# Group softmax on one core: tiles computed in place, twelve buffers, loads and stores on two queues

## The chip, the cores and the metric

The kernel runs on one NeuronCore of a Trainium2 chip; the other cores are idle. The metric is device time in microseconds, the median of three runs. The engines that matter here are VectorE (DVE in the profile), ScalarE (ACT), SyncE (SP, which only issues transfers) and the 16 DMA engines that move data between HBM and the on-chip memory, SBUF. An engine runs its instructions in order, and an instruction that waits holds up all that stand behind it on its engine.

## The reference

```python
def reference(x):                       # x: (4, 4096, 4352) float32
    B, N, D = x.shape
    G = 8
    Dg = D // G                         # 544
    x_g = x.reshape(B, N, G, Dg)
    x_g = x_g - x_g.max(axis=-1, keepdims=True)
    exp = np.exp(x_g)
    out = exp / exp.sum(axis=-1, keepdims=True)
    return out.reshape(B, N, D).astype(np.float32)
```

Each row of 4352 numbers falls into 8 groups of 544, and each group gets its own softmax. The input is 285 MB and the output is as large.

## The kernel before

The 16384 rows are cut into 128 tiles of 128 rows, one row to a partition; a tile is 128 x 4352 float32, 17408 bytes to a partition and 2176 KB in all. One loop runs over the tiles. For each tile SP loads `xt` (line 32); VectorE takes the 8 negated group maxima in one instruction, `mx` (line 35); ScalarE runs 8 activations (line 40), each of which writes the exponentials of one group into a second tile `ot` and their sum into a column of `sm`; VectorE takes the reciprocals `rs` (line 49) and multiplies each group of `ot` by its own (line 51); SP stores `ot` (line 52).

The pool has 4 buffers for each name, so 4 of `xt` and 4 of `ot`. A load of tile t+4 waits for ScalarE to have read tile t's `xt`, and an activation of tile t+4 overwrites an `ot` whose store must have landed. All loads and all stores are issued by SP, in one line of instructions. The framework orders the instructions of each engine itself, so the order on an engine is not that of the loop. It also tells DMAs apart by eight completion semaphores, DMAHW0 to DMAHW7, given out in turn; a DMA that is given a semaphore waits until the one that had it before has landed.

Of the kernel before, what the change touches and what calls it, by code (L numbers as in the profile page):

```python
# [1 line left out]

# [4 lines left out]


@with_exitstack
def kernel(  # L10
    ctx: ExitStack,
    tc: tile.TileContext,
    x: bass.AP,
    out: bass.AP,
):
    nc = tc.nc
    G = 8
    P = 128
    xf = x.flatten_outer_dims()
    of = out.flatten_outer_dims()  # L20
    N, D = xf.shape
    Dg = D // G
    xg = xf.rearrange("n (g d) -> n g d", g=G)
    og = of.rearrange("n (g d) -> n g d", g=G)
    ntiles = N // P

    pool = ctx.enter_context(tc.tile_pool(name="io", bufs=4))
    small = ctx.enter_context(tc.tile_pool(name="small", bufs=4))

    for t in range(ntiles):  # L30
        xt = pool.tile([P, G, Dg], mybir.dt.float32)
        nc.sync.dma_start(out=xt, in_=xg[t * P:(t + 1) * P])  # L32

        mx = small.tile([P, G], mybir.dt.float32)
        nc.vector.reduce_max(out=mx, in_=xt, axis=mybir.AxisListType.X, negate=True)  # L35

        sm = small.tile([P, G], mybir.dt.float32)
        ot = pool.tile([P, G, Dg], mybir.dt.float32)
        for g in range(G):
            nc.scalar.activation(  # L40
                out=ot[:, g, :],
                in_=xt[:, g, :],
                func=mybir.ActivationFunctionType.Exp,
                bias=mx[:, g:g + 1],
                scale=1.0,
                accum_out=sm[:, g:g + 1],
            )
        rs = small.tile([P, G], mybir.dt.float32)
        nc.vector.reciprocal(out=rs, in_=sm)  # L49
        for g in range(G):  # L50
            nc.vector.tensor_scalar_mul(out=ot[:, g, :], in0=ot[:, g, :], scalar1=rs[:, g:g + 1])  # L51
        nc.sync.dma_start(out=og[t * P:(t + 1) * P], in_=ot)  # L52


# [1 line left out]
_INS = ['x']  # L56
_OUTS = [((4, 4096, 4352), 'float32')]


# [23 lines left out]
```

## Time and profile before

| | us |
|---|---|
| median of 3 runs | 1601.17 (1600.88 to 1601.21) |
| the profiled execution: span from first to last instruction | 1599.5 |
| VectorE busy | 1048.2 (66%) |
| ScalarE busy | 760.8 (48%) |
| DMA engines, share of the span (queue q1) | 85.6% |
| DMA rate over the span | 357 GB/s |

The profiled execution's own time is not given beside its span; the span is 1.67 us under the median of the runs, and that difference is taken as what lies around it. Busy time is the time in which an engine works. The idle time in front of an instruction is put down to what ended it, the releaser. For a DMA, the profile gives the time from its issue to its landing, when the data is there and its semaphore has counted up. A transfer's rows are spread over all 16 DMA engines.

### The profile page before, as it was taken

What the parts mean: (1) busy time and instruction counts of PE and PEld (TensorE: products, weight loads), DVE (VectorE), ACT (ScalarE), POOL (GpSimd) and SP (SyncE); (2) the same over time, 40 slices, a digit from 0 to 9 for tenths busy, and PEclk for the clock granted to TensorE, in tenths of its full rate; (3) what the DMA queues carried; (4) which work ended last, traced back from release to release, by engine and by line L of the source; (5) the groups of instructions that cost most, each with busy time, mean ns of one, the idle gap of its engine ahead of it and who ended that gap; (6) DMA issues with size and microseconds to landing.
All of it is one profiled execution on the core that took longest, in us unless ns stands there. A gap on an engine that the chain in (4) does not pass through costs nothing.

```text
span 1599.5 us, 4255 instructions
## 1 busy us (share of the span) xinstructions
DVE 1048.2 (66%) x1280; ACT 760.8 (48%) x2049; POOL 0.2 (0%) x4
## 2 busy tenths in 40 slices
DVE  7568655587556775567765677656776567765566
ACT  6245444455444554445544355443554435544354
POOL 0000000000000000000000000000000000000000
DMA  8888998888988889888898888998889988898887
GB/s 362 355 341 349 376 383 346 337 349 369 390 348 341 349 355 390 361 337 353 351 383 369 341 349 355 374 378 336 344 359 376 376 342 341 362 375 371 344 340 312
DMA packets 36897, 570.71 MB, mean 357 GB/s; under 512 B 4096, under 2 KB 4096, under 8 KB 4096
## 3 DMA queue, kind: packets, MB, share of 16 engines
q1 hardware_dynamic: 36864, 570.44, 85.6%
q14 instruction: 33, 0.27, 0.0%
HBM read 285.21 MB, written 285.21 MB: 357 GB/s over the span
## 4 chain that ended last, share of the span: by engine, by line
DMA 33%; DVE 27%; ACT 26%; issue 10%; SPq 1%; DVEq 0%; ACTq 0%
DMA xt<-in_x_dram 33%; ACT ot L40 26%; DVE ot L51 18%; DVE mx L35 8%; DVE rs L49 1%; SPq L32 1%; SPq L52 1%; DVEq L78 0%; ACTq L78 0%
## 5 line engine op out<-in xcount | busy, mean ns | idle before, releaser
L40 ACT ACTIVATE ot<-xt,mx 128x544 f32<-128x544 f32 x1024 | 750.7, 734 | 817.8 <-DVE mx L35 667.3
L35 DVE TENSOR_REDUCE mx<-xt 128x8 f32<-128x4352 f32 x128 | 599.5, 4683 | 426.0 <-DMA xt<-in_x_dram 426.0
L51 DVE TENSOR_SCALAR ot<-ot,rs 128x544 f32<-128x544 f32 x1024 | 434.3, 499 | 4.5
L40 ACT ACTIVATION_READ_ACCUMULATOR ot<-xt,mx 128x1 f32 x1024 | 191.4, 187 | 0.0
L49 DVE RECIPROCAL rs<-sm 128x8 f32<-128x8 f32 x128 | 25.5, 199 | 113.3 <-ACT ot L40 113.3
L40 ACT ACT_TABLE_LOAD x1 | 1.3, 1283 | 9.7 <-DMA xt<-in_x_dram 9.7
L67 POOL MEMSET const-uint8-127<- 128x1 uint8 x1 | 0.1, 102 | 0.0
L67 POOL MEMSET const-bfloat16-1.0<- 128x1 bf16 x1 | 0.1, 101 | 0.0
L67 POOL MEMSET const-float32-0.0<- 128x1 f32 x1 | 0.1, 98 | 0.2 <-issue 0.2
L67 POOL MEMSET const-float32-1.0<- 128x1 f32 x1 | 0.1, 98 | 0.0
## 6 DMA issues: line engine op xcount, KB each, us to landing
xt<-in_x_dram SPq DMA_DIRECT2D x128, 2176.0 KB, 17.1
out_dram<-ot SPq DMA_DIRECT2D x128, 2176.0 KB, 6.6
```

Of the source, the lines that this page charges most:

```text
L32: nc.sync.dma_start(out=xt, in_=xg[t * P:(t + 1) * P])
L35: nc.vector.reduce_max(out=mx, in_=xt, axis=mybir.AxisListType.X, negate=True)
L40: nc.scalar.activation(out=ot[:, g, :], in_=xt[:, g, :], func=mybir.ActivationFunctionType.Exp, bias=mx[:, g:g + 1], scale=1.0, accum_out= ...
L49: nc.vector.reciprocal(out=rs, in_=sm)
L51: nc.vector.tensor_scalar_mul(out=ot[:, g, :], in0=ot[:, g, :], scalar1=rs[:, g:g + 1])
L52: nc.sync.dma_start(out=og[t * P:(t + 1) * P], in_=ot)
L67: nc = _bacc.Bacc("TRN2", target_bir_lowering=False, num_devices=1)
```

## The change

The exponentials are written over the tile that was loaded, and the scaled values over these, so the second tile is gone and the one pool has 12 buffers of the loaded tile. The order of the instructions is written out by hand: twelve loads first, then in each round the maximum and the exponentials of tile i, and the scaling and the store of tile i-1. Loads are issued by SP, stores by ScalarE. A load of tile i+12 takes the buffer of tile i and so waits for tile i's store to have landed. The arithmetic and the shapes of all instructions are as before.

```diff
+    NBUF = 12
-    pool = ctx.enter_context(tc.tile_pool(name="io", bufs=4))
+    pool = ctx.enter_context(tc.tile_pool(name="io", bufs=NBUF))
-    for t in range(ntiles):
-        xt = pool.tile([P, G, Dg], mybir.dt.float32)
-        nc.sync.dma_start(out=xt, in_=xg[t * P:(t + 1) * P])
+    def load(i):
+        xt = pool.tile([P, G, Dg], f32, name="xt")
+        tiles[i] = xt
+        nc.sync.dma_start(out=xt, in_=xg[i * P:(i + 1) * P])
-        mx = small.tile([P, G], mybir.dt.float32)
+    def store(i, eng):
+        eng.dma_start(out=og[i * P:(i + 1) * P], in_=tiles.pop(i))
+
+    def expo(i):
+        xt = tiles[i]
+        mx = small.tile([P, G], f32, name="mx")
         nc.vector.reduce_max(out=mx, in_=xt, axis=mybir.AxisListType.X, negate=True)
-        ot = pool.tile([P, G, Dg], mybir.dt.float32)
...
             nc.scalar.activation(
-                out=ot[:, g, :],
+                out=xt[:, g, :],
                 in_=xt[:, g, :],
...
+    def scale(i):
+        xt = tiles[i]
+        rs = small.tile([P, G], f32, name="rs")
+        nc.vector.reciprocal(out=rs, in_=sums.pop(i))
         for g in range(G):
-            nc.vector.tensor_scalar_mul(out=ot[:, g, :], in0=ot[:, g, :], scalar1=rs[:, g:g + 1])
-        nc.sync.dma_start(out=og[t * P:(t + 1) * P], in_=ot)
+            nc.vector.tensor_scalar_mul(out=xt[:, g, :], in0=xt[:, g, :], scalar1=rs[:, g:g + 1])
+
+    with tc.manual_schedule():
+        for i in range(NBUF):
+            load(i)
+        for i in range(nt + 1):
+            if i < nt:
+                expo(i)
+            if i:
+                scale(i - 1)
+                store(i - 1, nc.scalar)
+                if i - 1 + NBUF < nt:
+                    load(i - 1 + NBUF)
```

What SP issues in the middle of the kernel before, with the semaphores that each DMA waits for (DMAHW are those of DMAs, DVE and Activation those of the engines; the number in a name tells buffers apart):

```order
L32 DMA xt_686<-in_x_dram 128x4352 [waits DMAHW2_49,Activation_49]
L32 DMA xt_711<-in_x_dram 128x4352 [waits DMAHW3_49,Activation_49]
L32 DMA xt_736<-in_x_dram 128x4352 [waits DMAHW4_49,Activation_49]
L32 DMA xt_761<-in_x_dram 128x4352 [waits DMAHW5_49,Activation_49]
L52 DMA out_0_dram<-ot_691 128x4352 [waits DMAHW6_49,DVE_49]
L52 DMA out_0_dram<-ot_716 128x4352 [waits DMAHW7_49,DVE_49]
L52 DMA out_0_dram<-ot_741 128x4352 [waits DMAHW0_49,DVE_49]
L52 DMA out_0_dram<-ot_766 128x4352 [waits DMAHW1_49,DVE_49]
```

Four loads stand together, and behind them four stores that wait for VectorE. The same engine in the middle of the changed kernel:

```order
L37 DMA xt_1008<-in_x_dram 128x4352 [waits DMAHW7_49,DMAHW6_49,DVE_49]
L37 DMA xt_1032<-in_x_dram 128x4352 [waits DMAHW1_49,DMAHW0_49,DVE_49]
L37 DMA xt_1056<-in_x_dram 128x4352 [waits DMAHW3_49,DMAHW2_49,DVE_49]
L37 DMA xt_1080<-in_x_dram 128x4352 [waits DMAHW5_49,DMAHW4_49,DVE_49]
L37 DMA xt_1104<-in_x_dram 128x4352 [waits DMAHW7_49,DMAHW6_49,DVE_49]
```

SP now holds loads alone. Each waits for the load that had its semaphore four loads earlier (the odd numbers) and for the store that empties its buffer (the even ones). ScalarE's line in the changed kernel, some rounds later, with the store of each tile between the activations:

```order
L40 DMA out_0_dram<-xt_984 128x4352 [waits DMAHW4_49,DVE_49]
L49 ACTIVATE xt_1032,sm_1276<-xt_1032,mx_1274 128x544 [waits DMAHW1_49,DVE_49,Activation_49]
L49 ACTIVATE xt_1032,sm_1276<-xt_1032,mx_1274 128x544 x7
L40 DMA out_0_dram<-xt_1008 128x4352 [waits DMAHW6_49,DVE_49]
L49 ACTIVATE xt_1056,sm_1300<-xt_1056,mx_1298 128x544 [waits DMAHW3_49,DVE_49,Activation_49]
L49 ACTIVATE xt_1056,sm_1300<-xt_1056,mx_1298 128x544 x7
L40 DMA out_0_dram<-xt_1032 128x4352 [waits DMAHW0_49,DVE_49]
```

In the kernel before ScalarE issued no DMA. Now a store stands behind the exponentials of the next tile, waits for the scaling of its own tile and for the store four earlier, which had its semaphore, and holds up the exponentials behind it.

## Rows read from the trace of the kernel before

**Rows 1.** The page's head and part 1: busy us, share, instructions.

```profile
span 1599.5 us, 4255 instructions
DVE 1048.2 (66%) x1280; ACT 760.8 (48%) x2049; POOL 0.2 (0%) x4
```

**Rows 2.** The page's parts 3 and 6: DMA queues; a load's KB, us to landing.

```profile
q1 hardware_dynamic: 36864, 570.44, 85.6%
q14 instruction: 33, 0.27, 0.0%
...
xt<-in_x_dram SPq DMA_DIRECT2D x128, 2176.0 KB, 17.1
```

**Rows 3.** Waits, whole span: us in total, times, longest; SP's own last.

```profile
ACT ot L40 <- DVE mx L35: 667.3, 33, 21.6
DVE mx L35 <- DMA xt<-in_x_dram: 426.0, 64, 13.2
...
SPq L52 <- DVE ot L51: 1397.0, 127, 24.1
```

**Rows 4.** Timeline of SP from 500 to 560 us: start, us, what it issued.

```profile
499.97 6.50 SPq L52 DMA_DIRECT2D out_dram<-ot  x2
506.56 4.01 SPq L32 DMA_DIRECT2D xt<-in_x_dram  x4
533.38 22.77 SPq L52 DMA_DIRECT2D out_dram<-ot  x4
556.25 3.95 SPq L32 DMA_DIRECT2D xt<-in_x_dram  x4
```

**Rows 5.** Timeline of VectorE, same stretch, idle time before each in brackets.

```profile
518.97 4.69 DVE L35 TENSOR_REDUCE mx<-xt 128x8 f32<-128x4352 f32 x1 [12.85 <-DMA xt<-in_x_dram]
524.16 4.69 DVE L35 TENSOR_REDUCE mx<-xt 128x8 f32<-128x4352 f32 x1 [0.51 <-DMA xt<-in_x_dram]
...
529.97 3.39 DVE L51 TENSOR_SCALAR ot<-ot,rs 128x544 f32<-128x544 f32 x8
...
538.10 3.39 DVE L51 TENSOR_SCALAR ot<-ot,rs 128x544 f32<-128x544 f32 x8
...
546.23 3.39 DVE L51 TENSOR_SCALAR ot<-ot,rs 128x544 f32<-128x544 f32 x8
```

**Rows 6.** Windows of that stretch; the last two columns: DMA share, GB/s.

```profile
510.00:512.00 2.00, 0.00 (x0) 0.00 (x0) 0.00 (x0) 1.00 1.20 383
512.00:514.00 2.00, 0.00 (x0) 0.00 (x0) 0.00 (x0) 1.00 0.85 287
514.00:528.00 14.00, 8.52 (x2) 4.26 (x11) 0.00 (x0) 1.00 0.99 424
540.00:542.00 2.00, 2.00 (x5) 2.00 (x7) 0.00 (x0) 1.00 0.00 0
...
542.00:547.00 5.00, 4.96 (x4) 2.83 (x9) 0.00 (x0) 1.00 0.99 418
```

**Rows 7.** Line 52, issue to landing: the stores issued at 506.1 and 1585.9.

```profile
DMA to landing us min/median/max: 7.6/7.6/7.6
...
DMA to landing us min/median/max: 6.6/6.6/6.6
```

**Rows 8.** Chain of waits, the 16 ScalarE instructions of one tile: start, us.

```profile
546.17 5.97 ACT ot L40 x16
```

**Rows 9.** Timeline of the first 30 us.

```profile
0.73 2.80 SPq L32 DMA_DIRECT2D xt<-in_x_dram  x4
...
9.69 4.68 DVE L35 TENSOR_REDUCE mx<-xt 128x8 f32<-128x4352 f32 x1 [9.69 <-DMA xt<-in_x_dram]
...
26.04 0.19 ACT L40 ACTIVATION_READ_ACCUMULATOR ot<-xt,mx 128x1 f32 x1
```

**Rows 10.** Timeline of SP in the last 40 us.

```profile
1577.77 14.64 SPq L52 DMA_DIRECT2D out_dram<-ot  x3
```

**Rows 11.** Line 52 over the whole span: ns min/median/max of an issue.

```profile
L52 SPq DMA_DIRECT2D out_dram<-ot x128: 332/343/348, 24.1 to 1592.1; - x128
```

More of the change, by code (lines that the diff above doesn't have):

```diff
@@ L24 @@
     og = of.rearrange("n (g d) -> n g d", g=G)
-    ntiles = N // P
-    pool = ctx.enter_context(tc.tile_pool(name="io", bufs=4))
+    nt = N // P
+    pool = ctx.enter_context(tc.tile_pool(name="io", bufs=NBUF))
     small = ctx.enter_context(tc.tile_pool(name="small", bufs=4))
-    for t in range(ntiles):
-        xt = pool.tile([P, G, Dg], mybir.dt.float32)
-        nc.sync.dma_start(out=xt, in_=xg[t * P:(t + 1) * P])
-        mx = small.tile([P, G], mybir.dt.float32)
+    f32 = mybir.dt.float32
+    tiles = {}
+    sums = {}
+    def load(i):
[7 more added lines that the diff above has]
+        mx = small.tile([P, G], f32, name="mx")
         nc.vector.reduce_max(out=mx, in_=xt, axis=mybir.AxisListType.X, negate=True)
-        sm = small.tile([P, G], mybir.dt.float32)
-        ot = pool.tile([P, G, Dg], mybir.dt.float32)
+        sm = small.tile([P, G], f32, name="sm")
+        sums[i] = sm
         for g in range(G):
             nc.scalar.activation(
-                out=ot[:, g, :],
+                out=xt[:, g, :],
                 in_=xt[:, g, :],
@@ L47 @@
             )
-        rs = small.tile([P, G], mybir.dt.float32)
-        nc.vector.reciprocal(out=rs, in_=sm)
+    def scale(i):
+        xt = tiles[i]
+        rs = small.tile([P, G], f32, name="rs")
+        nc.vector.reciprocal(out=rs, in_=sums.pop(i))
         for g in range(G):
-            nc.vector.tensor_scalar_mul(out=ot[:, g, :], in0=ot[:, g, :], scalar1=rs[:, g:g + 1])
-        nc.sync.dma_start(out=og[t * P:(t + 1) * P], in_=ot)
+            nc.vector.tensor_scalar_mul(out=xt[:, g, :], in0=xt[:, g, :], scalar1=rs[:, g:g + 1])
[10 more added lines that the diff above has]
+                    load(i - 1 + NBUF)
 _INS = ['x']
```

## The prediction

> **What bounds the kernel now.** I read the engines' busy time first [rows 1]. VectorE works 1048 us and ScalarE 761 us of 1599.5, so neither is full. The DMA queue is at 85.6% [rows 2], which is high, and the question is whether the rest is overhead inside the transfers or time in which nothing is in flight. The windows answer it [rows 6]: between 514 and 528 us, when only loads are in flight, the 16 engines run at a share of 0.99 and 424 GB/s; between 540 and 542 us they move nothing at all; from 542 to 547 us one store alone runs at 0.99 and 418. The transfers are at a ceiling when there are any, and then there are none.
>
> What a transfer costs at that ceiling is read from VectorE's timeline [rows 5]: it is idle, and starts a maximum at 518.97 and the next at 524.16, each as its load lands. Loads queued back to back land 5.19 us apart. A load is 2176 KB [rows 2], so this is 429 GB/s, one percent above the 424 of the window; the store's 418 is within three percent of it, and I take 5.19 for both.
>
> Why the engines run dry is in SP's timeline [rows 4]. SP issues four loads at 506.56 and the next four at 556.25: a period of 49.69 us for four tiles. In between it issues stores one after another as VectorE finishes tiles, and the waits of SP say how long it stands there: 1397 us in all for line 51 [rows 3]. The next loads are queued behind those stores on SP. VectorE finishes tiles 8.13 us apart (529.97, 538.10, 546.23 in [rows 5]), a store needs only 5.19, and each leaves a gap. Eight transfers of 5.19 are 41.5 us of the 49.69; the other 8.2 us in each of 32 periods, 262 us in all, are what the kernel loses. Then the four loads come together, and VectorE waits 12.85 us for the first of them that it has not yet got. That is most of its 426 us of waiting for loads, and ScalarE's 667 us behind VectorE follows from it [rows 3].
>
> **The change part by part.** Loads no longer stand behind stores. From the written order a load waits for the load four earlier and for the store that empties its buffer, so up to four loads and four stores are in flight. A pair of transfers costs the DMA engines 2 x 5.19 = 10.38 us per tile. Compute needs less: VectorE 8.13 us, ScalarE 5.97 us for its 16 instructions [rows 8] and 0.34 us to issue a store [rows 11], so 6.3 us. The bound moves to the DMA engines as long as a load is always queued.
>
> Is one always queued? The loop that a buffer goes round is, if loads and stores share the engines evenly: four loads at 10.38 us from issue to landing, 41.5; the tile through compute, 14.4 us (load landed at 518.97, its store issued at 533.38 [rows 4, 5]) and 6 us more, since the store now stands behind the next tile's exponentials; four stores, 41.5, and 1.4 for a store's start (it lands 6.6 us after issue when it runs alone [rows 7], of which 5.19 is transfer). That is 105 us. Twelve buffers at 10.38 us give 124.6. So there are buffers to spare, and the spare time is where the added waits sit: a store on ScalarE that waits for an older store holds back the next exponentials, VectorE waits for those, and neither is late for the DMA engines. At the start the first nine loads need only loads to have landed; they keep the engines busy until about 4.5 + 9 x 5.19 = 51 us. The tenth waits for the first store; ScalarE is done with the second tile's exponentials at about 26.2 [rows 9], so that store lands by about 40 even at half rate.
>
> The in-place writes cost nothing that I can see: line 51 already works in place at 3.39 us for eight, and no engine reads the tile that another writes. The hand-written order on VectorE (maximum, then the scaling of the tile before) has the same instructions.
>
> The sum, for the profiled execution:
> - Data starts at 9.69 - 5.19 = 4.5 us [rows 9]: 4.5.
> - 256 transfers at 5.19: 1328.6.
> - The end. When no loads are left, VectorE delivers a tile every 8.13 us and a store takes 5.19, so each store that is not queued by then opens a gap of 2.94. Between none of these (enough stores queued) and twelve (35 us) I take two or three, since four stores are queued then and cover most of the rest: 7.5.
> - Instruction fetches, 0.27 MB [rows 2], now run against a full queue. On one engine alone (429 / 16 = 26.8 GB/s) they would be 10 us, spread over all 0.6; I take 5.
> - From the last store's landing to the end: the last store is issued at 1592.08 (the end of the last three less one issue of 0.33 [rows 10, 11]), lands 6.6 us later, and the span ends at 1599.5: 0.8.
>
> This is 1346.4 us of span, and with the 1.7 us between the span and the median of the runs 1348 us. Against 1599.5 it takes back the 262 us of idle DMA time and gives up some 10 at the end and to instruction fetches.
>
> **The unknown price: loads and stores at the same time.** The trace has almost no stretch of this kind, since one queue carries both in order. It has one junction per period: a store with a load queued right behind it. There the store lands 7.6 us after issue instead of 6.6 [rows 7], and the two windows around it run at 383 and 287 GB/s [rows 6]. So a change from writing HBM to reading it costs up to 1.0 us. In the changed kernel both queues hold work all the time. If the cost vanishes because reads and writes of both kinds overlap evenly, it is 0. If it is paid once for each pair of transfers it is 128 x 1.0 = 128 us, and if it is paid at each of the eight rows that a DMA engine moves of a transfer (36864 packets over 256 transfers and 16 engines are nine each, eight of data and one that signals) it is 1024 us. I take 0, by the row nearest to a full queue, the 424 GB/s at a share of 0.99, and because the junction looks like the emptying of one kind of work before the other has started. This is the weakest step.
>
> No run here shows loads and stores together on two queues; the Trainium skill does ("DMA: Bandwidth & Descriptors", Latency and other measured facts): copies of [128 x 16 KiB] tiles between HBM tensors on the sync and scalar queues run at 207 to 214 GB/s per direction. An estimate from that page's 428 GB/s for both directions would put the 570.44 MB at 1333 us, beside the 1328.6 above.
>
> **Rivals.**
> - Mixing costs a part: one junction for each pair, 128 us more, 1476 us; anything from 1375 to 1490 belongs here. For it speaks the 7.6 us store; against it that the load behind that store then lands at the usual 5.2 us (506.1 + 7.6 = 513.7, next landing 518.97 [rows 5]), so the stall is short and only once.
> - Slower: mixed traffic runs all the time as in the two junction windows, at their mean of 335 GB/s: 570.44 MB take 1703 us, and with the other 20 us 1722. The place is every DMA engine, at each row that follows one of the other direction. It decides below 361 GB/s (570.44 MB in 1601 less 20 us), or from 2.0 us of loss per pair. The junction's price seen so far is half of that, but per row it would be many times more.
> - A cap on the mean: the 357 GB/s of the span (570.44 MB in 1599.5 us) is itself the limit, faster stretches are bursts that are paid back, and the idle time was harmless. Nothing changes then but the two ends, 1601 to 1612 us. The 14 us at 424 GB/s speak against it, and so does an idle stretch that ends when VectorE finishes a tile. The Trainium skill ("SBUF — State Buffer", Summary: rules for kernel authors) says to plan with about 358 GB/s between HBM and SBUF, which would be an estimate of 1593 us for the bytes; the trace disagrees, with its 424.
> - Loads and stores together go faster than either alone, because one reads HBM while the other writes it. Each kind alone already keeps the engines at a share of 0.99 [rows 6], so I expect no more than a percent or two: 1325.
>
> **How the numbers follow.** The forecast, 1348 us, has 0.62; its own range is 1335 to 1375 (end and fetches by their bounds, up to 0.2 us per pair of mixing cost). Mixing in part has 0.18, the slower case 0.11, the cap 0.04, the gain 0.05. Faster than 1598 are the forecast, the partial cost and the gain, 0.85; the measurement tells 0.2%, 3 us, from no change, and 0.03 falls within it (the cap, or a mixing cost that happens to eat all); slower is the rest, 0.12. The range that leaves out no more than 2 in 10 goes from 1330 to 1490: it holds the forecast and nearly all of the partial cost.
>
> **What would show it.** In the changed kernel the DMA share should be 0.97 or more in every slice but the first and last, and the rate 420 to 430. Maxima on VectorE should start 10.4 us apart on average, most of its waits put down to loads or to ScalarE, with ScalarE waiting for stores. Loads and stores should each take about 40 us from issue to landing, since four of each are queued. If slices show a share near 1 with a rate well under 420, mixing has a price; if the share falls under 0.95 in the middle, loads ran out and the loop of twelve buffers was too short. A tail of over 50 us after the last load would put the end term wrong.

## The result, and the profile after

The changed kernel takes 1342.75 us (1342.72 to 1342.9) against 1601.15 us, a ratio of 0.8387 with a 95% interval of 0.8375 to 0.8399. The forecast was 1348, with a range of 1330 to 1490. Its profiled execution has a span of 1341.1 us.

The page of the changed kernel: head, engines' busy time, DMA share and rate in 40 slices, queues, and the issues with KB and us to landing.

```profile
span 1341.1 us, 4111 instructions
DVE 1046.1 (78%) x1280; ACT 763.9 (57%) x2049; POOL 0.2 (0%) x4
...
DMA  9999999999999999999999999999999999999996
GB/s 389 431 432 430 431 431 432 431 431 431 430 431 431 431 431 431 432 432 431 432 431 430 432 429 432 431 431 431 431 431 431 431 432 431 431 432 432 431 386 294
...
q1 hardware_dynamic: 18432, 285.22, 49.7%
q10 hardware_dynamic: 18432, 285.22, 49.6%
q14 instruction: 32, 0.26, 0.0%
...
xt<-in_x_dram SPq DMA_DIRECT2D x128, 2176.0 KB, 33.8
out_dram<-xt ACTq DMA_DIRECT2D x128, 2176.0 KB, 41.2
```

VectorE and ScalarE work as long as before, to within 3.1 us [rows 1]; only the span is shorter. Where the DMA engines stood at 85.6% in one queue [rows 2], two queues now hold them at 49.7 and 49.6%, and the rate is 431 GB/s in nearly every slice but the ends. A load takes 33.8 us from issue to landing instead of 17.1 and does no harm by it: the queue is long, not slow.

VectorE in the middle, idle time before each instruction in brackets, and then SP and ScalarE's sequencer in the same stretch:

```profile
600.94 4.68 DVE L45 TENSOR_REDUCE mx<-xt 128x8 f32<-128x4352 f32 x1
608.40 0.20 DVE L61 RECIPROCAL rs<-sm 128x8 f32<-128x8 f32 x1 [2.78 <-ACT xt L49]
608.64 3.39 DVE L63 TENSOR_SCALAR xt<-xt,rs 128x544 f32<-128x544 f32 x8
611.95 4.68 DVE L45 TENSOR_REDUCE mx<-xt 128x8 f32<-128x4352 f32 x1
...
601.91 20.94 SPq L37 DMA_DIRECT2D xt<-in_x_dram  x3
...
601.93 0.35 ACTq L40 DMA_DIRECT2D out_dram<-xt  x1
612.25 0.35 ACTq L40 DMA_DIRECT2D out_dram<-xt  x1
622.55 0.35 ACTq L40 DMA_DIRECT2D out_dram<-xt  x1
```

Before, four loads and then four stores were issued in turn every 49.69 us [rows 4]. Now a store and a load go out every 10.3 us, side by side. VectorE's instructions take what they took [rows 5]; it never waits 12.85 us for a load any more, but two or three for ScalarE in every round.

The waits of the engines (total, times, longest), SP's own last:

```profile
ACT xt L49 <- DMA out_dram<-xt: 418.1, 94, 5.0
DVE rs L61 <- ACT xt L49: 271.1, 102, 25.7
ACT xt L49 <- DMA xt<-in_x_dram: 83.4, 6, 28.0
...
DVE mx L45 <- DMA xt<-in_x_dram: 11.8, 4, 9.5
...
SPq L37 <- DMA out_dram<-xt: 1093.4, 108, 19.4
```

The 426 us that VectorE waited for loads [rows 3] are 11.8. What waits is ScalarE, in the middle for a store that had the same semaphore four stores earlier, and VectorE behind it. SP still stands for 1093 us, as it did before for 1397; but now it stands with three or four loads already handed over (33.8 us each, at one per 10.3). Long waiting meant starved transfers in one kernel and a full queue in the other, so the DMA share decides which it is.

The end, in windows (the last two columns are DMA share and GB/s):

```profile
1260.00:1290.00 30.00, 22.94 (x30) 23.74 (x64) 0.00 (x0) 1.00 1.01 431
1290.00:1300.00 10.00, 9.93 (x13) 6.30 (x17) 0.00 (x0) 1.00 0.91 390
1300.00:1310.00 10.00, 9.96 (x16) 7.83 (x22) 0.00 (x0) 1.00 0.67 284
1310.00:1320.00 10.00, 9.96 (x15) 7.83 (x23) 0.00 (x0) 1.00 0.59 251
1320.00:1330.00 10.00, 7.47 (x10) 7.83 (x22) 0.00 (x0) 1.00 0.73 308
1330.00:1341.00 11.00, 3.59 (x9) 0.02 (x1) 0.00 (x0) 1.00 0.78 329
```

Before 1290 the rate is 431 GB/s at a share of 1.01, against 424 at 0.99 in the best stretch before [rows 6]. From there VectorE is full, and the DMA engines wait for it: 0.9 + 3.3 + 4.1 + 2.7 + 2.4 = 13.4 us of idle time, a mean over engines that don't all have the same left to do (below).

### The profile page after: what moved, and what is told of

The parts are those of the page before. It is cut to its first block, busy times and chain, and to the rows that moved or that the text cites. A ratio compares the mean times of both kernels' runs of the same rounds, so it can differ in the third digit from the quotient of the medians.

```text
span 1341.1 us, 4111 instructions
## 1 busy us (share of the span) xinstructions
DVE 1046.1 (78%) x1280; ACT 763.9 (57%) x2049; POOL 0.2 (0%) x4
## 3 DMA queue, kind: packets, MB, share of 16 engines
q1 hardware_dynamic: 18432, 285.22, 49.7%
q10 hardware_dynamic: 18432, 285.22, 49.6%
## 4 chain that ended last, share of the span: by engine, by line
DMA 87%; DVE 8%; ACT 2%; issue 2%; SPq 0%; ACTq 0%; DVEq 0%
DMA out_dram<-xt 74%; DMA xt<-in_x_dram 13%; DVE xt L63 4%; DVE mx L45 3%; ACT xt L49 2%; SPq L37 0%; DVE rs L61 0%; ACTq L40 0%; DVEq L103 0%; ACTq L49 0%
## 5 line engine op out<-in xcount | busy, mean ns | idle before, releaser
L49 ACT ACTIVATE xt<-xt,mx 128x544 f32<-128x544 f32 x1024 | 751.0, 734 | 556.6 <-DMA out_dram<-xt 418.1
L45 DVE TENSOR_REDUCE mx<-xt 128x8 f32<-128x4352 f32 x128 | 598.8, 4678 | 11.8 <-DMA xt<-in_x_dram 11.8
L63 DVE TENSOR_SCALAR xt<-xt,rs 128x544 f32<-128x544 f32 x1024 | 434.1, 498 | 4.7 <-DVE rs L61 0.2
L49 ACT ACTIVATION_READ_ACCUMULATOR xt<-xt,mx 128x1 f32 x1024 | 191.3, 187 | 0.0
## 6 DMA issues: line engine op xcount, KB each, us to landing
xt<-in_x_dram SPq DMA_DIRECT2D x128, 2176.0 KB, 33.8
out_dram<-xt ACTq DMA_DIRECT2D x128, 2176.0 KB, 41.2
```

What stands on the lines that cost most here:

```text
L49: nc.scalar.activation(out=xt[:, g, :], in_=xt[:, g, :], func=mybir.ActivationFunctionType.Exp, bias=mx[:, g:g + 1], scale=1.0, accum_out= ...
L63: nc.vector.tensor_scalar_mul(out=xt[:, g, :], in0=xt[:, g, :], scalar1=rs[:, g:g + 1])
```

## The experiments

Each kernel ran beside the kernel before on one chip (1600.6 to 1600.8 us there).

**Loads freed from the stores by one line.** In the kernel before, stores go to ScalarE's queue.

```diff
-        nc.sync.dma_start(out=og[t * P:(t + 1) * P], in_=ot)
+        nc.scalar.dma_start(out=og[t * P:(t + 1) * P], in_=ot)
```

> The kernel before with one edit: stores are issued by ScalarE instead of SP; 4 + 4 buffers and the framework's own order stay. Theory (the gain is the loads set free from behind the stores on SP): loads need only the exponentials of four tiles earlier, which run ahead of the DMA engines, so the DMA share goes to 0.98 or more and the time to 1335 to 1360 us. Rival (the twelve in-place buffers are what fills the gaps): most of the idle DMA time stays, 1500 us or more.

Measured: 1379.33 us, ratio 0.8619 (0.8605 to 0.8633). Its page:

```profile
DMA  9999999999999999999999999999999999999997
GB/s 391 406 413 425 421 415 417 420 424 413 420 422 414 413 421 421 419 415 416 424 412 416 421 416 418 420 423 413 421 423 418 414 420 414 421 416 419 421 414 314
...
xt<-in_x_dram SPq DMA_DIRECT2D x128, 2176.0 KB, 11.0
out_dram<-ot ACTq DMA_DIRECT2D x128, 2176.0 KB, 8.9
```

Most of the gain, 221 of 258 us, comes with this one line. It is not the queue alone: the framework orders the instructions anew for this kernel, and VectorE now takes the maximum and the scaling of tiles in turn throughout, where it did two maxima in a row in every four tiles before [rows 5]. The time is above what I had expected, and the reason is in the rate: a share of 0.9 and more in every slice but the last, but 415 GB/s on average over the span instead of 426. With 11.0 and 8.9 us to landing, about one load and one store are in flight at a time. The engines are busy, and slower.

**One queue, twelve buffers.** The changed kernel with stores back on SP.

```diff
-                store(i - 1, nc.scalar)
+                store(i - 1, nc.sync)
```

> The changed kernel with one edit: stores go back to SP, so one queue carries all in order; 12 in-place buffers stay. Theory (one in-order queue is what starves the DMA engines): the load of tile i+12 waits on SP for the store issued just before it, and by then the queue is empty, so each pair costs 2 x 5.16 plus 1.4 us of a store's start, 11.8 to 12 us, in all 1480 to 1530 us. Rival (buffers alone): 1345 us.

Measured: 1891.01 us, ratio 1.1817 (1.18 to 1.1835), 18% slower than before. The direction is the theory's, the size is not. SP's issues, and then windows with DMA share and GB/s last:

```profile
742.92 0.33 SPq L37 DMA_DIRECT2D xt<-in_x_dram  x1
743.29 0.43 SPq L40 DMA_DIRECT2D out_dram<-xt  x1
758.86 0.33 SPq L37 DMA_DIRECT2D xt<-in_x_dram  x1
```

```profile
712.00:716.00 4.00, 3.96 (x10) 3.30 (x9) 0.00 (x0) 1.00 0.54 137
...
728.00:732.00 4.00, 1.93 (x5) 4.00 (x12) 0.00 (x0) 1.00 0.96 322
732.00:736.00 4.00, 0.00 (x0) 0.44 (x2) 0.00 (x0) 1.00 0.95 305
736.00:740.00 4.00, 2.22 (x1) 0.00 (x0) 0.00 (x0) 1.00 1.00 431
```

One load and one store go out every 15.9 us here (14.8 on average, 1891 / 128), where I had 11.8. The queue runs empty each time, as expected (the 137). But then the engines, with one load and one store queued, run at a share of 0.95 and only 305 to 322 GB/s, and the load issued at 742.92 lands after 10.7 us. I had 6.6 for it, 1.4 to start and 5.17 to move, which is a store's time. The next two rows are from issue to landing of line 37 of this kernel from 700 to 1700 us, and of the first load of the kernel before, with no store near it:

```profile
DMA to landing us min/median/max: 8.5/10.3/11.2
...
DMA to landing us min/median/max: 8.9/8.9/8.9
```

So a load takes 8.9 us without any store about, and the fastest loads here take no longer. The trace also has the landing on each of the 16 DMA engines; these are the first, the eighth (called the middle one below) and the last, in us after issue:

```
first load of the kernel before         6.9   7.5   8.9
a store alone there, issued at 541.52   6.4   6.5   6.6
load issued at 742.92                   8.1   8.4  10.7
store issued at 743.29                 12.9  13.2  15.6
```

On the middle engine the store lands 5.17 us after the load, so nothing is lost between the two. The 4.1 us that this load takes beyond 6.6 are three things. Its middle engine would land 1.0 us later than a store's even with no store about (7.5 against 6.5); it lands 0.9 later here than that (8.4); and the slowest engine is another 2.3 behind, where a store's is 0.1. The lag stays with the store, and the next load has to wait for it. Only the 0.9 looks like the 1.0 us of [rows 7], so about 1 us per pair can be put down to a change of direction here, not 4. Why one engine is so late, by 1.5 us in a first load without any store and by 2.3 here, stays open.

**One queue, but deep.** As the last kernel, with the load that follows a store fetching the tile eight ahead, not twelve.

```diff
+    AHEAD = 8
...
-        for i in range(NBUF):
+        for i in range(AHEAD):
...
-                store(i - 1, nc.scalar)
-                if i - 1 + NBUF < nt:
-                    load(i - 1 + NBUF)
+                store(i - 1, nc.sync)
+                if i - 1 + AHEAD < nt:
+                    load(i - 1 + AHEAD)
```

> As the kernel with one queue and 12 in-place buffers, but a load follows the store of the tile eight before it, not twelve, so that it waits for a store that is four older and the queue stays four pairs deep. Every store is followed by a load in one queue: 128 junctions. Theory (a junction in a full queue costs nothing, since with two queues the rate was 431 GB/s): 1335 to 1350 us and no slices under 425 GB/s; then a second queue isn't needed at all. Rival (the 1.0 us of the store at the junction before is the price of each change of direction in one queue): 1341 + 128 = 1470 us, near 390 GB/s.

Measured: 1342.35 us, ratio 0.8385 (0.8372 to 0.8397), the changed kernel's time from one queue. Its queue and issues from the page, and then two windows of the start:

```profile
q1 hardware_dynamic: 36864, 570.44, 99.5%
...
xt<-in_x_dram SPq DMA_DIRECT2D x128, 2176.0 KB, 41.8
out_dram<-xt SPq DMA_DIRECT2D x128, 2176.0 KB, 41.7
```

```profile
40.00:50.00 10.00, 9.96 (x12) 7.79 (x23) 0.00 (x0) 1.00 1.00 404
...
60.00:70.00 10.00, 9.93 (x14) 6.78 (x19) 0.00 (x0) 1.00 1.01 430
```

All stores but the last eight have a load behind them in one queue, 120 junctions, and after the first (the 404) the rate shows no cost of any. The rival with 1.0 us for each is out for a deep queue, and so is the idea that the second queue is what helps.

**How many buffers.** NBUF = 8, 5 and 4 in the changed kernel, nothing else edited.

```diff
-    NBUF = 12
+    NBUF = 8
```

> The changed kernel with 8 buffers instead of 12. Theory A (what ends late is the slowest DMA engine: three of the 16 land the last store 11 to 14 us after the others in the one-queue kernel, so the end cannot come before about 1339): 1339 to 1344 us, no gain from a shorter backlog of compute. Theory B (what ends late is compute: 12 tiles leave some six of them to be worked off at 8.13 us each after the last load): with 8 buffers fewer are left, and the time falls by 8 to 12 us to 1331 to 1335. Theory C (the prediction's loop of 105 us is a need, not a queue that shrinks): 105 / 8 = 13.1 us per tile, 1690 us.

> The changed kernel with 5 buffers. The least loop of a buffer is a load at half rate 10.3 + 1.4, compute 14.4 + 6, a store at half rate 10.3 + 1.4, 44 us; five buffers at 10.31 give 51.6, so it should still be bound by the DMA engines: 1335 to 1350 us. Rival (a shallow queue brings back the price of changing direction, 1.0 us or more for a pair): 1400 us or more.

> The changed kernel with 4 buffers. Four at 10.31 give 41.2 us, under the least loop of 44: 128 x 44 / 4 = 1408 us, with stores and loads that no longer wait for one another somewhat less, 1385 to 1420. With the price of changing direction in a shallow queue on top (1.0 us per pair and more): 1500 us or more.

Measured: 8 buffers 1339.02 us, 5 buffers 1341.96, 4 buffers 1403.66 (ratios 0.8363, 0.8382, 0.8781, each to 0.0025 at most). The rates of the page, for 8, 5 and 4 buffers (one fence each):

```profile
GB/s 389 430 430 432 432 431 432 431 432 430 432 430 432 431 431 431 432 431 431 431 431 433 430 431 431 432 430 432 431 432 430 432 430 432 430 431 431 431 432 307
```

```profile
GB/s 389 423 432 432 431 431 431 430 432 430 430 431 432 429 430 430 426 427 429 430 426 428 430 429 426 429 429 429 428 429 428 426 427 428 430 428 428 431 429 319
```

```profile
GB/s 353 377 405 399 420 403 409 422 412 415 412 412 414 401 415 419 414 413 414 414 419 405 401 414 405 419 416 399 420 409 415 400 405 416 417 412 417 415 399 342
```

Five buffers are nearly enough. Theory C of the 8-buffer kernel is out: the 105 us that I had counted round the loop are the length of a full queue, and shrink with it. Four buffers come out near the 44 us of their least loop, 128 x 44 / 4 = 1408. But the DMA share does not fall with them (51.0 and 48.3% on the two queues); the rate does, to some 410 GB/s. Whether the loop binds or the transfers are slower in so short a queue was not tried apart. Eight buffers come out at the lower edge of theory A, yet 3.7 us under twelve, so theory B had a part too.

**The transfers alone, and the instructions alone.** First the 256 transfers with all computation left out; then the same with the computation's instructions put back on 4 elements of each group.

```diff
-        for i in range(nt + 1):
-            if i < nt:
-                expo(i)
-            if i:
-                scale(i - 1)
-                store(i - 1, nc.scalar)
-                if i - 1 + NBUF < nt:
-                    load(i - 1 + NBUF)
+        for i in range(nt):
+            store(i, nc.scalar)
+            if i + NBUF < nt:
+                load(i + NBUF)
```

> Leaves all computation out: the same 128 loads on SP and 128 stores on ScalarE's queue, 12 buffers. Theory (the middle is DMA alone and the end is late compute): 4.3 us of start, 1323.5 us for the bytes at 431 GB/s, and an end of a few us, 1329 to 1335 us; 8 to 13 us less than the changed kernel. Rival (the end costs the same without compute, or compute slows the transfers): within 3 us of 1342.7, or under 1320.

```diff
+    scr = small.tile([P, G, 4], f32, name="scr")
...
-        nc.vector.reduce_max(out=mx, in_=xt, axis=mybir.AxisListType.X, negate=True)
+        nc.vector.reduce_max(out=mx, in_=xt[:, :, 0:4], axis=mybir.AxisListType.X, negate=True)
...
-                out=xt[:, g, :],
-                in_=xt[:, g, :],
+                out=scr[:, g, :],
+                in_=xt[:, g, 0:4],
...
-            nc.vector.tensor_scalar_mul(out=xt[:, g, :], in0=xt[:, g, :], scalar1=rs[:, g:g + 1])
+            nc.vector.tensor_scalar_mul(out=scr[:, g, :], in0=scr[:, g, :], scalar1=rs[:, g:g + 1])
```

> Leaves the computation out but keeps its instructions: the same number on VectorE and ScalarE, each on 4 elements of a group instead of 544, so the output is a copy of the input. The copy without instructions took 1331.05 us. Theory A (instruction fetches run on three DMA engines, and these come last): the lag of the slowest engines at the end grows from 2 to 3 us to 10 us or more, 1339 to 1343 us. Rival (compute on large operands is what delays those engines): 1331 to 1333 us and a lag of 3 us.

Measured: 1331.05 us without instructions, 1338.97 with them, ratios 0.8315 (0.8302 to 0.8327) and 0.8365 (0.8352 to 0.8377). The first kernel's page, its span and instruction queue, and the second's span:

```profile
span 1329.5 us, 540 instructions
...
q14 instruction: 4, 0.03, 0.0%
...
span 1337.1 us, 4094 instructions
```

A store counts up its semaphore once for each of the 16 DMA engines that has landed its share. These are the times of the last store in the trace, in us, engine by engine in order of time:

```
transfers alone                1325.6 1325.6 1325.6 1325.7 1325.7 1325.7 1325.8 1325.8 1325.8 1325.8 1325.9 1326.0 1326.0 1326.6 1327.3 1328.7
with small instructions        1325.8 1325.8 1325.8 1325.8 1325.9 1325.9 1325.9 1326.0 1326.0 1326.1 1326.1 1326.4 1326.8 1334.3 1335.2 1336.3
one queue, deep, full work     1325.4 1325.6 1325.6 1325.6 1325.7 1325.7 1325.7 1325.8 1326.0 1326.3 1327.8 1328.3 1329.1 1336.4 1338.3 1339.6
```

Thirteen engines are done by 1326.8 us without or with the small instructions, and by 1329.1 with the full work. With instructions, three come last, 8 to 10 us after the middle ones with small operands and 11 to 14 with large. So 4094 instructions against 540 go with 7.9 us. Large operands can carry no more than the 3.4 us from there to the deep single queue (1342.35), and the 8-buffer kernel with the full work, 1339.02, takes no longer than the small instructions; the rival is out as the main cause.

That it is the fetching and not something else about the instructions can be followed in the trace. The kernel without computation fetches only four blocks of 8 KB while it runs, at 383.4, 423.4, 1043.6 and 1084.2 us. How far the slowest engine lands a store behind the middle one is 1.1 to 1.2 us for stores that land from 375 to 416.5 us and 1.8 for the next, at 426.9; it goes from 2.35 to 3.0 across the last fetch; and the second slowest goes from 0.95 to 1.4 across the third. Three of four fetches put one engine back by 0.5 to 0.7 us for good. The changed kernel makes 32 fetches, and there the slowest engine falls behind all the time: 1.0 us at 143 us, 4.5 at 659, 9.4 at 1176. No kernel varied the fetches and nothing else.

**Twelve and eight on one chip, and fewer instructions.** The last three ran together; the third makes the eight multiplications of a tile one.

```diff
-    NBUF = 12
+    NBUF = 8
...
-        for g in range(G):
-            nc.vector.tensor_scalar_mul(out=xt[:, g, :], in0=xt[:, g, :], scalar1=rs[:, g:g + 1])
+        nc.vector.tensor_tensor(out=xt, in0=xt, in1=rs.unsqueeze(2).to_broadcast([P, G, Dg]), op=mybir.AluOpType.mult)
```

> The changed kernel again, unedited, so that it stands beside the 8-buffer kernels on one chip: 1341 to 1344 us.

> The 8-buffer kernel again, beside the 12-buffer one: 3 to 5 us less than it if the earlier difference (1339.0 against 1342.75, on different calls) is the backlog of compute at the end; within 1.5 us of it if that was the chip.

> 8 buffers, and the eight multiplications of a tile made one that reads the reciprocals along a stretched axis: 128 instructions of VectorE for 1024, some 900 of 4121 fewer. VectorE should need some 4.6 us for one (its maximum over as many elements takes 4.68), 9.5 us per tile, still under 10.31. Theory (instruction fetches delay the three slowest DMA engines): their lag falls by a fifth or more and the time to 1335 to 1338 us. Rival (VectorE at 9.5 us per tile makes the end later, since the last tile's scaling takes 1.2 us longer and a backlog shrinks by 0.8 us per tile only): 1339 to 1345 us.

Measured: 12 buffers 1342.9 us, ratio 0.8389 (0.8377 to 0.84); 8 buffers 1338.58, 0.8361 (0.8349 to 0.8372); 8 buffers with one multiplication 1339.45, 0.8368 (0.8356 to 0.8379). Eight buffers beat twelve by 4.3 us on one chip (3.7 above, in separate runs), and are the fastest of all kernels that do the whole work. Of the third kernel:

```profile
span 1338.1 us, 3343 instructions
...
q14 instruction: 27, 0.21, 0.0%
...
L62 DVE TENSOR_TENSOR xt<-xt,rs 128x4352 f32<-128x4352 f32 x128 | 600.6, 4692 | 4.4
```

778 instructions fewer than the 8-buffer kernel's 4121 did not make it faster, and the theory's 1335 to 1338 us was missed. The rival's range was met, but not for the rival's reason: the last store goes out at 1326.7 us, against 1326.5 in the 8-buffer kernel. Its last load lands on thirteen engines by 1298.6 us, and on the other three at 1303.2, 1305.4 and 1310.9; in the 8-buffer kernel those were 1308.1, 1310.4 and 1312.0. Two of the late engines came nearer and the latest hardly moved, and the time is that of the latest. Which instructions that one engine fetches was not found out.

## Why the prediction was right

**The step that carried it** was that the idle DMA time, 262 us, is caused by loads queued behind stores and can be taken back whole. The store-to-ScalarE kernel bears out the first half, 221 us with one edited line and the framework's new order; the rest came with a deeper queue. Not all of the 262 us were idle, though: a share of 85.6% leaves 230 us of the span idle, and the remainder is about what 1.0 us at each of 32 junctions [rows 7] comes to. The window that had been read as a ceiling, 424 GB/s, was near one, and the mean over the span, 357, was not: the cap is refuted by 429 to 432 GB/s in 37 of 40 slices.

**The terms of the sum.** Data started at 9.49 - 5.17 = 4.3 us; I had 4.5. The transfers are 570.44 MB at 431 GB/s, 1323.5 us or 256 x 5.17, where I had 5.19 and 1328.6: this is the term that was off, by 5.1 us, and nearly the whole 5.3 between the forecast span and the measured one. What is left for the end, the fetches and the last landing is 1341.1 - 4.3 - 1323.5 = 13.3 us, and my three terms made 13.3. That they agree to the tenth is luck, for the parts are others than I had. Instructions were worth 7.9 us between the two kernels without computation, where I had 5, and eight buffers for twelve some 4, where I had 7.5 for the backlog; but these are differences between other kernels and no split of this one. In the changed kernel the last store lands on all 16 engines between 1340.1 and 1340.3 us, so the late engines do not set its end directly. VectorE does, and the late engines act on it through a load (below).

**The weakest step**, 0 for loads and stores together, came out right for this kernel, and my reason for it was only half of one. The price exists: it was 1.0 us for a store with loads behind it and about as much for a pair in the shallow single queue, and the 4 + 4-buffer kernel with two queues ran at a rate 3% lower. In the changed kernel and in the deep single queue it was paid once, at the first change (20 to 30 us in the changed kernel, 40 to 50 above), and then no more:

```profile
20.00:30.00 10.00, 9.73 (x15) 7.56 (x23) 0.00 (x0) 1.00 1.01 395
```

Why a full queue makes it free, these runs don't show. It is not that the engines drift apart and turn each at its own time: the last load lands on the 16 engines from 1573.3 to 1573.7 us in the kernel before, and on twelve of them from 1273.9 to 1274.4 in the changed one, so most turn together there too. The slower rival was wrong for this kernel, and the 1891 us of the shallow single queue do not bear it out either: there the queue ran empty after every pair, and what can be put down to the change of direction is about 1 us per pair, not something at every row.

**The loop of twelve buffers** was argued with numbers of a full queue, 105 us against 124.6. The conclusion held, for a reason that was too strict: eight buffers at 82.5 us are as full, and only with four, at 41.2 us, is the kernel slower. Two of the waits that I had called harmless, ScalarE for old stores and VectorE for ScalarE, are so in the middle but not at the end. VectorE's longest wait in the changed kernel:

```profile
1266.96 0.20 DVE L61 RECIPROCAL rs<-sm 128x8 f32<-128x8 f32 x1 [25.74 <-ACT xt L49]
```

ScalarE stands there for 28.0 us until a load lands (the waits above), of a tile that it gets to only later. While loads and stores alternate, a store takes over the semaphore of an older store. When the loads run out, the stores get all eight semaphores in turn, and by the trace the store of tile 117 gets the one of the load of tile 124. That load is on the middle engine at 1249.1 us and on the slowest, one of the three late ones, at 1260.4; the store goes out at 1260.5, and the exponentials behind it after that. From then on VectorE is the bound: it scales the last nine tiles 8.13 us apart, the very last 6.2, while the DMA engines idle. In the 8-buffer kernel ScalarE's longest wait for a load is 11.4 us, which fits its 4 us less, but this was not tried apart.

**What I had asked of the profile**: a share of 0.97 or more in all slices but the first and last (1.01 in the middle; the last slice but one falls short, at 386 GB/s), 420 to 430 GB/s (431), stores at about 40 us to landing (41.2; loads 33.8), a tail of no more than 50 us after the last load (1291.4 to 1341.1, 49.7; thirteen of the 16 engines had it by 1276.0).

## What to carry to other kernels

Find a stretch where the transfers are saturated and one where nothing moves before believing a mean rate; the gap between the two is what a change of order can win. What fills it is not a second queue or many buffers as such but work always queued on the DMA engines: one queue with the right order did as well as two, one with the wrong order lost 18%. Once the queue is full, more buffers need not help: eight were 0.3% faster than twelve here. Look at the end by itself, where the loads run out: a store that takes over the semaphore of a load waits for that load, and holds up the engine that issues it.

## What the runs showed of the hardware that I had not expected

- A DMA share of 0.95 went with 305 to 322 GB/s while one load and one store were queued at a time; the same engines moved 431 GB/s at a share of 1.01 when several of each were queued.
- One core sustained 431 GB/s of loads and stores together for 1.2 ms, no less than loads alone (429).
- The first load of the kernel before, into idle engines, landed 8.9 us after its issue; a store of the same size alone landed after 6.6.
- Instructions cost DMA time: with 4094 instead of 540, three of the 16 engines landed the last store 8 to 10 us after the others, and the kernel took 7.9 us more. At three of the four fetches of the kernel with 540, one engine fell back by 0.5 to 0.7 us.
